# Squared token factors where MLP results are added, and both halves of the tokens in one 512-column matmul

## The chip, the cores and the metric

The kernel runs on one core of one Trainium2 chip. The metric is device time in microseconds (us) of one execution of the whole program; the profile is that of one execution. Engines: TensorE (PE; its weight loads are shown apart as PEld), VectorE (DVE), ScalarE (ACT), GpSimd (POOL), and SyncE (SP), which here only issues DMAs.

## The reference

A decoder trunk of two layers for 256 tokens of width 2048, in float32. Each layer is a mixer (first a gated linear recurrence, then dilated attention) and an MLP; each of the four blocks norms its input and adds its result to the residual `x`:

```python
def _rmsnorm(x, g):
    y = x32 * lax.rsqrt(jnp.mean(x32 * x32, axis=-1, keepdims=True) + EPS)
    return (y * g.astype(jnp.float32)).astype(x.dtype)

def _mlp(h, w1, w2):
    u = jnp.einsum('bsd,df->bsf', h, w1)
    u = jnp.square(jax.nn.relu(u))
    return jnp.einsum('bsf,fd->bsd', u, w2)

x = x + _mlp(_rmsnorm(x, mlp_norm[i]), mlp_w1[i], mlp_w2[i])
```

`w1` is 2048 x 8192, `w2` 8192 x 2048. The norm's factor of a token, call it r, is one number for each token. Since it is positive, relu(r v)^2 = r^2 relu(v)^2, and `w2` acts within a token, so the factor may come in before the relu, as r, or at the end, as r squared.

## The kernel before

**Precision.** A float32 product is made of three products in a faster format: each operand is cut into a high part (`hilo`, `hi_piece`: ACT copies and rounds) and a low part (`lo_piece`: DVE subtracts the high part), and high x high, high x low and low x high are added up in PSUM. The weights come from HBM in units of 1 MB (128 x 2048); `cut_hi` (line 132) and `cut_lo` (line 136) cut each one. There are three buffers for high parts, so the high cut of unit i+3 waits until PE has read the high part of unit i for the last time. The high cut is issued right behind an item (`behind_unit`), the low cut two units ahead (`before_unit`).

**Order.** The program is a list of items, in most cases one weight unit each. For every item the loop at the end issues what must be ready before, then the item's matmuls, then the next high cut, then what was put off to this item: `after(n, fn)` runs `fn` n items later. Each engine works through its instructions in exactly the order in which they were issued; a waiting instruction holds all those behind it on its engine.

**The MLP.** `plan_mlp` goes through 8 parts of 1024 hidden columns. For each part there are eight *first products*, one for each 128 of its hidden columns (`plan_first`, `stand_w`): 16 blocks of 128 inputs, and for each the high weights by the tokens' high part, the high weights by the low part, and the low weights by the high part, three matmuls of 256 columns. The tokens (`xT`) are not normed here, only multiplied by the norm's gains. `u_done` (line 592) takes the sum from PSUM on DVE: relu, times the tokens' factors, which `rstd_rows` has spread over all partitions by two transposes on PE and a copy on ACT. ACT squares it and copies the high part; `u_low` makes the low part one item later.

The *second products* of parts 0 to 6 are made by a scheme with fewer multiplications: a 2 x 2 block product (two token halves, two halves of the part's hidden columns, two chunks of 512 outputs) with seven products instead of eight, on sums of tokens (`sums_of_tokens`, DVE) and sums of weights (line 682 on DVE, and DMAs that add, issued by POOL). Each product is 12 matmuls of 512 columns. Where a product is finished, `take` (line 686) adds it to or takes it from the residual `xc` on DVE. Part 7 goes the plain way (`plan_plain`, `add_x`).

First products of part p+1 are interleaved with second products of part p in an order written out by hand (`ORDER`). Numbered, with W1 to W8 for the first products, it is for each part:

```
W1, b11 0, t1 0, W2, b21 0, b22 0, t2 0, W3, t3 0, W4, t4 0, b11 1, t1 1, W5,
b22 1, t2 1, W6, t3 1, b21 1, W7, W8, t4 1
```

"0" and "1" are the two pairs of output chunks. Seven parts of each of the two MLPs have this form (in part 0, t1 0 and W2 change places), so there are 14 of them, and 12 steps from one to the next. `b22 1` goes on adding in the bank that `t1 1` has written, after its take. A part's token sums are made after `t3 1` of the part before and, for the last pair of hidden columns, after `t4 1`.

**Banks.** A first product writes 256 of the 512 columns of its PSUM bank. For part 0 these are `acc` banks (four, lines with `acc`), later `g` banks (two, used in turn).

`stand_both` is used by the attention for its heads: for each 128 inputs, one matmul of 512 columns has the high weights by both parts of the tokens, and one of 256 the low weights by the high part; `qk_done` copies the half with the low part on ACT and `qk_sum` adds the other.

`add_x`, `close_chunk` and `final_add` add a block's finished result to the residual; `rstd_cols` works out the factors by token (`rs`), one column for each half of the tokens.

Of the kernel before, what the change touches and what calls it, by code (L numbers as in the profile page):

```python
# [9 lines left out]

F32 = mybir.dt.float32
F32R = mybir.dt.float32r
# [10 lines left out]
HD = 128  # L23
DFF = 8192
EPS = 1e-6
KD = D // 128
KR = DR // 128
NCH = D // 512
# [48 lines left out]
def trunk(ctx: ExitStack, tc: tile.TileContext, a: dict, out: bass.AP):  # L77
# [113 lines left out]
    def after(n, fn, *args):  # L191
        later.setdefault(now[0] + n, []).append((fn, args))
# [79 lines left out]
    def new_ssq():  # L272
        state["ssq"] = perm.tile([P, NT, NCH], F32, name="ssq", bufs=2)

    def rstd_cols():
        v = perm.tile([P, 4, NT], F32, name="rs", bufs=2)
        nc.vector.tensor_reduce(v[:, 0, :], state["ssq"], axis=AX.X, op=OP.add)
        nc.vector.tensor_scalar(v[:, 0, :], v[:, 0, :], 1.0 / D, EPS, op0=OP.mult, op1=OP.add)
        nc.scalar.activation(v[:, 1, :], v[:, 0, :], AF.Sqrt)
        nc.vector.reciprocal(v[:, 2, :], v[:, 1, :])  # L280
        nc.vector.tensor_mul(v[:, 3, :], v[:, 2, :], v[:, 2, :])
        nc.vector.tensor_mul(v[:, 3, :], v[:, 3, :], v[:, 0, :])
        nc.vector.tensor_scalar(v[:, 3, :], v[:, 3, :], -0.5, 1.5, op0=OP.mult, op1=OP.add)
        nc.vector.tensor_mul(v[:, 2, :], v[:, 2, :], v[:, 3, :])
        state["rstd"] = v[:, 2, :]

    def rstd_rows():
        state["kick"] = True
# [22 lines left out]
            mm(ps, hi[:, s], xl, False, False)  # L311
            mm(ps, lo[:, s], xh, False, last and j == len(ks) - 1)

    def stand_both(ps, u):

        hi, lo = split[u]
        state["kick"] = False
        for k in range(KD):
            x, s = xT(k), slice(k * 128, (k + 1) * 128)
            mm(ps, hi[:, s], x.rearrange("p (t u q) -> p u q t", t=2, u=2), k == 0, False)  # L320
            mm(ps[:, :S], lo[:, s], moving(x, 0), False, k == KD - 1)

# [42 lines left out]
        for t in range(NT):  # L365
            nc.vector.tensor_add(xc[n][:, t, :], xc[n][:, t, :], acc[t])

    def close_chunk(n, gname, rows):
        def closed(acc):
            if n == 0:  # L370
                new_ssq()
            add_x(n, acc)
            if n < NCH - 1:
                square_sum(n)
            after(1, transpose_chunk, n, gname)
            if n == NCH - 1:
                after(1, square_sum, n)
                after(1, rstd_cols)
                if rows:
                    after(4, rstd_rows)  # L380
        return closed
# [142 lines left out]
    def plan_rec():  # L524
        def proj(h, j, g):
            u = unit(a["w_in"][(KR if g else 0) + 2 * h + j] if len(units) >= FIRST else a["w_first"][len(units)])

            done = gb_done if g else xb_done
            if u < FIRST:
                first[u] = (done, h, j)  # L530
                return

            bank = []

            def begin():
                bank.append(acc_tile() if u > ROWS + 1 else psum.tile([P, 512], F32, name="g" if u <= ROWS else "tr", bufs=2))
                if u == ROWS:
                    stand_w(bank[0][:, :S], u, range(0, HEAD), 0, True, False)
                    state.pop("rows")()

            def run():
                if u != ROWS:
                    begin()
                at = HEAD if u == ROWS else 0
                stand_w(bank[0][:, :S], u, range(at, KD), at, at == 0, True)
                if u == ROWS - 1:
                    first.append((done, h, j, bank[0]))
                else:
                    after(0, done, h, j, bank[0])
            if u == ROWS:  # L550
                item(None, begin)
            item(u, run)

        def gate(h):
            u = unit(a["w_g"][h], 1024)
            item(u, lambda: gate_run(h, u))

        def oproj(n, kq):
            u = unit(a["w_out"][n * 5 + kq])
            out_item(("o", n), u, aT, range(4 * kq, 4 * kq + 4), kq == 0, kq == 4,  # L560
                     close_chunk(n, "mlp0", True))

        for h in range(NB):
            proj(h, 0, 0)
            proj(h, 1, 0)
            proj(h, 0, 1)
            proj(h, 1, 1)
            if h:
                gate(h - 1)
        for kq in (0, 1, 2):  # L570
            oproj(0, kq)
        gate(NB - 1)
        oproj(0, 3)
        for kq in (0, 1, 2, 3):
            oproj(1, kq)
        oproj(0, 4)
        oproj(1, 4)
        for n in (2, 3):
            for kq in range(5):
                oproj(n, kq)  # L580
# [6 lines left out]
    def u_done(p, j, ps):  # L587
        h, k = divmod(j, 4)
        if h == 0:
            squares[p, k] = lru.tile([P, 2, S], F32, name="uu", bufs=4)  # L590
        uu = squares[p, k][:, h, :]
        nc.vector.scalar_tensor_tensor(uu, ps[:, :S], 0.0, state["rstdB"], op0=OP.max, op1=OP.mult)
        nc.scalar.activation(uu, uu, AF.Square)
        t = new_aT(8 * (p % 2) + j)
        nc.scalar.activation(t[:, 0:256], uu, AF.Copy)
        after(1, u_low, t, uu)
        if h == 1 and GROUPS[p]:
            after(1, waiting.append, (p, k))

    def u_low(t, uu):  # L600
        nc.vector.tensor_sub(t[:, 256:512], uu, t[:, 0:256].bitcast(F32))
# [36 lines left out]
    def plan_mlp(w1, w2, done):  # L638
        def plan_first(p, j):
            u = unit(w1[8 * p + j])  # L640

            def run():
                accs["u", p, j] = acc_tile() if p == 0 else psum.tile([P, 512], F32, name="g", bufs=2)
                stand_w(accs["u", p, j][:, :S], u, range(KD), 0, True, True)
                after(0, u_done, p, j, accs.pop(("u", p, j)))
            item(u, run, "w")

        def plan_start():
            us = [unit(w1[j]) for j in (0, 4)]
            for at, ks in enumerate((range(0, 12), range(12, 16))):  # L650
                for u, j in zip(us, (0, 4)):
                    def run(u=u, j=j, ks=ks, at=at):
                        if at == 0:
                            accs["u", 0, j] = acc_tile()
                        stand_w(accs["u", 0, j][:, :S], u, ks, ks[0], at == 0, at == 1)
                        if at == 1:
                            after(1 if j == 0 else 0, u_done, 0, j, accs.pop(("u", 0, j)))
                    item(u, run)

        def plan_plain(p, n, h, last_part):  # L660
            u = unit(w2[((p // 2) * 4 + n) * 4 + (p % 2) * 2 + h])
            out_item(("m", n), u, aT, range(8 * (p % 2) + 4 * h, 8 * (p % 2) + 4 * h + 4), h == 0, h == 1,
                     done(n) if last_part else (lambda acc, n=n: add_x(n, acc)))

        def plan_group(p, n0, last_group):

# [15 lines left out]
                nc.vector.tensor_add(q[to], q[a], q[b])  # L682

            def take(n, t, b, sign):
                x = xc[n0 + n][:, t, :]
                (nc.vector.tensor_add if sign > 0 else nc.vector.tensor_sub)(x, x, bank[b])

            def product(name, loads, source, what, b, first, takes):
                def load_all():
# [197 lines left out]
    def plan_att():  # L887
        def v(g, kq):
            u = unit(a["w_v"][g * 4 + kq])
            out_item(("v", g), u, xT, range(4 * kq, 4 * kq + 4), kq == 0, kq == 3, lambda acc: v_done(g, acc))  # L890

        def head(h):
            for w in range(2):
                def run(u=unit(a["w_qk"][NH * w + h]), w=w):
                    ps = acc_tile()
                    stand_both(ps, u)
                    after(0, qk_done, h, w, ps)
                item(len(units) - 1, run, "w")

        for kq in (0, 1, 2):  # L900
            v(0, kq)
        for kq in (0, 1, 2):
            v(1, kq)
        v(0, 3)
        v(1, 3)
        for h in range(NH):
            if h == NH // 2:
                for g in (2, 3):
                    for kq in range(4):
                        v(g, kq)  # L910
            head(h)

        def oproj(n, kq):
            u = unit(a["w_o"][n * 4 + kq])
            out_item(("a", n), u, aT, range(4 * kq, 4 * kq + 4), kq == 0, kq == 3, close_chunk(n, "mlp1", True))

        for n in (0, 1):
            for kq in (0, 1, 2):
                oproj(n, kq)
        oproj(0, 3)  # L920
        oproj(1, 3)
        for n in (2, 3):
            for kq in range(4):
                oproj(n, kq)


    def final_done(n):
        def done(acc):
            if n == 0:
                new_ssq()  # L930
            add_x(n, acc)
            square_sum(n)
            nc.gpsimd.tensor_mul(xc[n], xc[n], state["gB"][:, None, n * 512:(n + 1) * 512].to_broadcast([P, NT, 512]))
            if n == NCH - 2:
# [11 lines left out]
    def final_add(acc, bank, cols, square, t=0):  # L946

        x = xc[LAST][:, t, cols]
        nc.vector.tensor_add(x, x, acc[bank][:, cols])
        junk = perm.tile([P, 512], mybir.dt.bfloat16, name="junk")  # L950
        nc.scalar.activation(junk[:, cols], x, AF.Square, accum_out=square)

# [88 lines left out]
    plan_rec()  # L1041
    item(None, lru.close)
    item(None, lambda: lru.open("mlp"))
    plan_mlp(a["w1_0"], a["w2_0"], lambda n: close_chunk(n, "mix1", True))
    item(None, lru.close)
    item(None, open_att)
    plan_att()
# [196 lines left out]
```

## Time and profile before

| | us |
|---|---|
| median of 3 runs | 2014.77 (2014.06 to 2015.1) |
| the profiled execution | 2014.87 |
| its span, first to last instruction | 2013.1 |
| granted TensorE clock, mean | 0.998 of full speed |
| weight cuts, high (ACT, 2048 wide) | 1.92 each |
| weight cuts, low (DVE, 2048 wide) | 2.29 each |
| line 592, relu and factor (DVE) | 0.42 each, 128 of them |
| line 686, takes (DVE) | 0.68 each, 150 of them |

The first MLP begins at about 357 us of the span and the second at about 1362; each lasts some 650 us. A row of the timeline gives the start and the length in us, the engine, the line, the operation, the tile written and those read; in square brackets stands how long the engine was idle before, and what ended the wait. A row of the groups ends with the busy time in us, the mean in ns and the idle time before. A row of a source line gives the least, the median and the longest duration in ns and the first and last start. PE's instructions overlap, so the start of one to the start of the next is what one costs; the same goes for DVE and ACT, where it is some 0.08 us less than the duration.

### The profile page before, as it was taken

To read this page: it belongs to the slowest core of one execution; us is meant where nothing else is said; L and a number is where in the kernel's file an instruction comes from. 1 tells how busy PE (TensorE), PEld (TensorE's weight loads), DVE (VectorE), ACT (ScalarE), POOL (GpSimd) and SP (SyncE) were. 2 spreads that over 40 slices of the span, in tenths; PEclk is the share of its full clock that TensorE was granted. 3 is DMA by queue.
4 is the path that set the end of the run, shared out by engine and by line. 5 is a ranking of instruction groups with operands and counts; after the bars stand their busy time and mean duration, and the time that the engine had idled before them with its cause. 6 is when DMAs were issued, how large, how long until landed. Compare 5 with 4: busy or idle time off the path is not lost.

```text
span 2013.1 us, 32932 instructions
## 1 busy us (share of the span) xinstructions
PE 2001.9 (99%) x13761; PEld 1876.5 (93%) x13761; DVE 1721.5 (86%) x1903; ACT 1294.2 (64%) x1420; POOL 87.9 (4%) x83
## 2 busy tenths in 40 slices
PE   9999999999999999999999999999999999999998
PEld 8999988999999999999889999889999999999997
DVE  7999865699999999998658969857999999999985
ACT  7878875566566666665657657656666666666664
POOL 0111110000000000000000000000000000000001
PEclk9999999999999999999999999999999999999999
DMA  8555565688788788787555555456887887887774
GB/s 311 205 195 201 190 225 189 244 258 251 251 287 264 234 288 274 247 250 250 201 210 180 184 194 179 177 194 245 251 251 258 287 269 226 294 276 243 251 242 164
DMA packets 68917, 472.54 MB, mean 235 GB/s; under 512 B 7584, under 2 KB 7712, under 8 KB 13472
## 3 DMA queue, kind: packets, MB, share of 16 engines
q1 hardware_dynamic: 60416, 411.18, 54.3%
q0 software_dynamic: 8064, 58.72, 14.8%
q8 instruction: 108, 1.77, 0.3%
q10 hardware_dynamic: 288, 0.52, 0.1%
q14 instruction: 41, 0.34, 0.0%
HBM read 409.58 MB, written 2.10 MB: 205 GB/s over the span
## 4 chain that ended last, share of the span: by engine, by line
PE 96%; DVE 3%; ACT 0%; issue 0%; DMA 0%; SPq 0%; ACTq 0%
PE acc L201 46%; PE g L201 32%; PE tr L201 18%; DVE wlo L136 1%; PE tr L242 1%; DVE c L437 0%; DMA raw<-in_w_first 0%; ACT whi L132 0%; PE tr L855 0%; DVE c L433 0%; DVE sT L625 0%; DVE qT L682 0%; DVE gw L462 0%; ACT xc L973 0%; DVE i L515 0%
## 5 line engine op out<-in xcount | busy, mean ns | idle before, releaser
L132 ACT ACTIVATE whi<-raw 128x2048 fp32r<-128x2048 f32 (+1 forms) x309 | 568.9, 1844 | 308.8 <-PE acc L201 166.1
L136 DVE TENSOR_TENSOR wlo<-raw,whi 128x2048 fp32r<-128x2048 f32 (+1 forms) x309 | 677.7, 2196 | 94.3 <-ACT whi L132 94.0
L201 PE MATMUL g<-xT,whi 128*128 128x256 f32 x3649 | 617.0, 275 | 0.0
L201 PEld LDWEIGHTS g<-xT,whi 128*128 128x128 f32 x3649 | 554.0, 192 | 0.0
L201 PE MATMUL g<-xT,wlo 128*128 128x256 f32 x1824 | 502.9, 276 | 0.2 <-DVE wlo L136 0.2
L201 PE MATMUL acc<-xT,whi 128*128 128x256 f32 (+1 forms) x2212 | 455.3, 300 | 0.7 <-ACT whi L132 0.7
L201 PE MATMUL acc<-xT,wlo 128*128 128x256 f32 x1360 | 373.3, 274 | 0.7 <-DVE wlo L136 0.6
L201 PEld LDWEIGHTS acc<-xT,whi 128*128 128x128 f32 x2212 | 355.5, 191 | 15.1 <-ACT whi L132 1.8
L201 PEld LDWEIGHTS g<-xT,wlo 128*128 128x128 f32 x1824 | 350.1, 192 | 1.5 <-DVE wlo L136 0.4
L201 PE MATMUL acc<-whi,aT 128*128 128x512 f32 (+1 forms) x1086 | 322.9, 374 | 0.0
L136 DVE TENSOR_TENSOR wlo<-q,whi 128x2048 fp32r<-128x2048 f32 x112 | 255.9, 2285 | 28.0 <-ACT whi L132 27.8
L132 ACT ACTIVATE whi<-q 128x2048 fp32r<-128x2048 f32 x112 | 214.6, 1917 | 79.4 <-PE g L201 52.3
L201 PEld LDWEIGHTS acc<-xT,wlo 128*128 128x128 f32 x1360 | 261.1, 192 | 1.6 <-DVE wlo L136 1.5
L201 PEld LDWEIGHTS acc<-whi,aT 128*128 128x128 f32 x1086 | 204.0, 189 | 27.6
L201 PE MATMUL tr<-whi,sT 128*128 128x512 f32 (+1 forms) x728 | 212.7, 364 | 0.0
L201 PE MATMUL acc<-wlo,aT 128*128 128x512 f32 (+1 forms) x536 | 200.8, 376 | 0.0
L132 ACT ACTIVATE whi<-qT 128x2048 fp32r<-128x2048 f32 x56 | 107.5, 1919 | 127.8 <-PE g L201 93.3
L201 PEld LDWEIGHTS tr<-whi,sT 128*128 128x128 f32 x728 | 137.6, 189 | 20.5
L201 PE MATMUL tr<-whi,aT 128*128 128x512 f32 (+1 forms) x462 | 140.3, 373 | 0.0
L136 DVE TENSOR_TENSOR wlo<-qT,whi 128x2048 fp32r<-128x2048 f32 x56 | 128.0, 2286 | 1.3 <-ACT whi L132 1.3
L201 PE MATMUL tr<-wlo,sT 128*128 128x512 f32 x336 | 127.4, 379 | 0.0
L201 PEld LDWEIGHTS acc<-wlo,aT 128*128 128x128 f32 x536 | 101.1, 189 | 13.2
(170 smaller groups left out, 2144.4 us busy)
## 6 DMA issues: line engine op xcount, KB each, us to landing
raw<-in_w SPq DMA_DIRECT2D x172, 1024.0 KB, 7.0
q<-in_w SPq DMA_DIRECT2D x84, 1024.0 KB, 8.1
raw<-in_w_in SPq DMA_DIRECT2D x35, 1024.0 KB, 4.8
raw<-in_w_qk SPq DMA_DIRECT2D x32, 1024.0 KB, 4.8
q<-q POOLq DMA_DIRECT2D x28, 1024.0 KB, 12.5
q<-qT POOLq DMA_DIRECT2D x28, 1024.0 KB, 7.6
raw<-in_w_out SPq DMA_DIRECT2D x20, 1024.0 KB, 4.8
raw<-in_w_v SPq DMA_DIRECT2D x16, 1024.0 KB, 4.8
```

Source lines behind the costliest of these rows:

```text
L132: nc.scalar.activation(split[i][0][:, s], r, AF.Copy)
L136: nc.vector.tensor_sub(split[i][1][:, s], r, split[i][0][:, s].bitcast(F32))
L201: nc.tensor.matmul(o, l, r, start=start, stop=stop, skip_group_check=True)
L242: nc.tensor.transpose(tr[:, k, t * 128:(t + 1) * 128], xc[n][:, t, c:c + 128], ident)
```

## The change

Two things change in both MLPs.

The first product is made by `stand_both`, 32 matmuls instead of 48, into all 512 columns of its bank. Line 592 becomes three steps in two items: ACT copies the half with the tokens' low part to `uu`, right behind the matmuls; DVE adds the other half and cuts below at zero (TENSOR_ADD_SAT, an operation of DVE's own table: the sum of two tensors, cut above and below at two constants); in the next item ACT squares and makes the high part, and one item after that DVE makes the low part.

The tokens' factors no longer come in there. `rstd_cols` squares them instead (two more small operations, the second for the negative), and every place where an MLP result is added to the residual multiplies by the factor of the token: `take`, the plain adds, the chunk's last add and the final adds. `rstd_rows` is no longer called ahead of the MLPs.

```diff
-    def rstd_cols():
-        v = perm.tile([P, 4, NT], F32, name="rs", bufs=2)
+    def rstd_cols(squared=False):
+        v = perm.tile([P, 6, NT], F32, name="rs", bufs=2)
...
+        if squared:
+            nc.vector.tensor_mul(v[:, 4, :], v[:, 2, :], v[:, 2, :])
+            nc.vector.tensor_scalar(v[:, 5, :], v[:, 4, :], -1.0, None, op0=OP.mult)
+            state["rstd2"] = v[:, 4:6, :]
...
-    def stand_both(ps, u):
+    def stand_both(ps, u, ks=range(KD)):
...
-        for k in range(KD):
+        for k in ks:
...
+    def add_scaled(x, acc, t, sign=1):
+
+        i = 0 if sign > 0 else 1
+        nc.vector.scalar_tensor_tensor(x, acc, state["rstd2"][:, i, t:t + 1], x, op0=OP.mult, op1=OP.add)
+
+    def add_mlp(n, acc):
+        for t in range(NT):
+            add_scaled(xc[n][:, t, :], acc[t], t)
+
-    def close_chunk(n, gname, rows):
+    def close_chunk(n, gname, add):
+        rows = add is add_mlp
+
...
-            add_x(n, acc)
+            add(n, acc)
...
-                after(1, rstd_cols)
+                after(1, rstd_cols, not rows)
                 if rows:
                     after(4, rstd_rows)
...
     def u_done(p, j, ps):
...
-        nc.vector.scalar_tensor_tensor(uu, ps[:, :S], 0.0, state["rstdB"], op0=OP.max, op1=OP.mult)
+        nc.scalar.activation(uu, ps[:, S:], AF.Copy)
+        after(0, u_sum, p, j, ps, uu)
+
+    def u_sum(p, j, ps, uu):
+        nc.vector._custom_dve(TENSOR_ADD_SAT, out=uu, in0=ps[:, :S], in1=uu, s0=LARGEST, s1=0.0)
+        after(1, u_square, p, j, uu)
+
+    def u_square(p, j, uu):
+        h, k = divmod(j, 4)
         nc.scalar.activation(uu, uu, AF.Square)
         t = new_aT(8 * (p % 2) + j)
         nc.scalar.activation(t[:, 0:256], uu, AF.Copy)
         after(1, u_low, t, uu)
         if h == 1 and GROUPS[p]:
-            after(1, waiting.append, (p, k))
+            waiting.append((p, k))
...
-                stand_w(accs["u", p, j][:, :S], u, range(KD), 0, True, True)
-                after(0, u_done, p, j, accs.pop(("u", p, j)))
+                stand_both(accs["u", p, j], u)
+                u_done(p, j, accs.pop(("u", p, j)))
...
             def take(n, t, b, sign):
-                x = xc[n0 + n][:, t, :]
-                (nc.vector.tensor_add if sign > 0 else nc.vector.tensor_sub)(x, x, bank[b])
+                add_scaled(xc[n0 + n][:, t, :], bank[b], t, sign)
...
     def final_add(acc, bank, cols, square, t=0):
...
-        nc.vector.tensor_add(x, x, acc[bank][:, cols])
+        add_scaled(x, acc[bank][:, cols], t)
```

The first two first products of an MLP, each made in two items (`plan_start`), change in the same way.

More of the change, by code (lines that the diff above doesn't have):

```diff
@@ L9 @@
 from concourse._compat import with_exitstack
+from concourse.dve_ops import TENSOR_ADD_SAT
 F32 = mybir.dt.float32
@@ L25 @@
 EPS = 1e-6
+LARGEST = float(np.finfo(np.float32).max)
 KD = D // 128
@@ L560, in oproj @@
             out_item(("o", n), u, aT, range(4 * kq, 4 * kq + 4), kq == 0, kq == 4,
-                     close_chunk(n, "mlp0", True))
+                     close_chunk(n, "mlp0", add_x))
         for h in range(NB):
@@ L654, in run @@
                             accs["u", 0, j] = acc_tile()
-                        stand_w(accs["u", 0, j][:, :S], u, ks, ks[0], at == 0, at == 1)
+                        stand_both(accs["u", 0, j], u, ks)
                         if at == 1:
-                            after(1 if j == 0 else 0, u_done, 0, j, accs.pop(("u", 0, j)))
+                            u_done(0, j, accs.pop(("u", 0, j)))
                     item(u, run)
@@ L662, in plan_plain @@
             out_item(("m", n), u, aT, range(8 * (p % 2) + 4 * h, 8 * (p % 2) + 4 * h + 4), h == 0, h == 1,
-                     done(n) if last_part else (lambda acc, n=n: add_x(n, acc)))
+                     done(n) if last_part else (lambda acc, n=n: add_mlp(n, acc)))
         def plan_group(p, n0, last_group):
@@ L914, in oproj @@
             u = unit(a["w_o"][n * 4 + kq])
-            out_item(("a", n), u, aT, range(4 * kq, 4 * kq + 4), kq == 0, kq == 3, close_chunk(n, "mlp1", True))
+            out_item(("a", n), u, aT, range(4 * kq, 4 * kq + 4), kq == 0, kq == 3, close_chunk(n, "mlp1", add_x))
         for n in (0, 1):
@@ L930, in done @@
                 new_ssq()
-            add_x(n, acc)
+            add_mlp(n, acc)
             square_sum(n)
@@ L1043, in trunk @@
     item(None, lambda: lru.open("mlp"))
-    plan_mlp(a["w1_0"], a["w2_0"], lambda n: close_chunk(n, "mix1", True))
+    plan_mlp(a["w1_0"], a["w2_0"], lambda n: close_chunk(n, "mix1", add_mlp))
     item(None, lru.close)
```

## The prediction

> **What bounds the kernel now.** I read the page first, then the waits, then one period of the MLP on the timeline of each engine.
>
> ```profile
> PE 2001.9 (99%) x13761; PEld 1876.5 (93%) x13761; DVE 1721.5 (86%) x1903; ACT 1294.2 (64%) x1420; POOL 87.9 (4%) x83
> PE 96%; DVE 3%; ACT 0%; issue 0%; DMA 0%; SPq 0%; ACTq 0%
> ```
>
> TensorE (PE) is busy 99% of the span and carries 96% of the chain that ended last, so over the whole span a shorter matmul stream is worth its full length. The table by stretches shows how near a second engine is in the stage that changes:
>
> ```profile
> 500.00:600.00 100.00, 100.00 (x704) 94.29 (x703) 93.33 (x82) 63.33 (x53) 4.28 (x5) 1.00 0.81 268
> ```
>
> The columns are PE, PEld, DVE, ACT, POOL. VectorE (DVE) works 93.33 of 100 us there, ScalarE (ACT) 63.33. The idle 7% is not spread evenly: it lies behind two of the eight first products of a part, W3 and W6. From each, DVE runs without a pause until PE itself waits for it. I call these **stretch A** (end of W3 to product b22 1) and **stretch C** (end of W6 to W2 of the next part). Stretch A on the timelines of PE, ACT and DVE:
>
> ```profile
> 509.78 0.38 PE L201 MATMUL tr<-whi,sT 128*128 128x512 f32 x1
> 509.87 1.91 ACT L132 ACTIVATE whi<-q 128x2048 fp32r<-128x2048 f32 x1 [3.32 <-PE g L201]
> 509.98 0.42 DVE L592 SCALAR_TENSOR_TENSOR uu<-g,rstdB 128x256 f32<-128x256 f32 x1 [0.71 <-PE g L201]
> 511.81 2.29 DVE L136 TENSOR_TENSOR wlo<-q,whi 128x2048 fp32r<-128x2048 f32 x1 [1.41 <-ACT whi L132]
> 530.12 0.68 DVE L686 TENSOR_TENSOR xc<-xc,tr 128x512 f32<-128x512 f32 x1
> 530.76 0.28 PE L201 MATMUL g<-xT,wlo 128*128 128x256 f32 x1
> 530.95 0.45 PE L201 MATMUL tr<-whi,sT 128*128 128x512 f32 x1
> ```
>
> W3 ends at 509.78. The high cut that needs its weight buffer starts then on ACT; DVE takes the low cut at its end (511.81), runs on to a take that ends at 530.80, and PE, which would have begun b22 1 0.11 us after 530.76, begins at 530.95: it waited 0.08 us for that take, whose bank b22 1 adds to. Stretch C:
>
> ```profile
> 541.57 0.38 PE L201 MATMUL tr<-whi,sT 128*128 128x512 f32 x1
> 541.66 1.92 ACT L132 ACTIVATE whi<-raw 128x2048 fp32r<-128x2048 f32 x1 [3.32 <-PE g L201]
> 543.61 2.29 DVE L136 TENSOR_TENSOR wlo<-raw,whi 128x2048 fp32r<-128x2048 f32 x1 [1.41 <-ACT whi L132]
> 568.59 2.28 DVE L136 TENSOR_TENSOR wlo<-raw,whi 128x2048 fp32r<-128x2048 f32 x1
> 570.92 0.38 PE L201 MATMUL g<-xT,wlo 128*128 128x256 f32 x1
> ```
>
> W6 ends at 541.57; DVE's run ends with the low cut of W2 at 570.87, and PE uses it at 570.92, its first use, a wait of about 0.08 us like that in A. Both come back in every part; first and last of 14 for A and of 12 for C:
>
> ```profile
> 451.43 0.45 PE L201 MATMUL tr<-whi,sT 128*128 128x512 f32 x1
> 1933.85 0.45 PE L201 MATMUL tr<-whi,sT 128*128 128x512 f32 x1
> 491.40 0.38 PE L201 MATMUL g<-xT,wlo 128*128 128x256 f32 x1
> 1894.31 0.38 PE L201 MATMUL g<-xT,wlo 128*128 128x256 f32 x1
> ```
>
> So PE and DVE are level to a tenth of a microsecond at 26 places. PE time saved inside A or C is a wait there, and time added to these two runs is paid in full. That decides the change.
>
> **What PE saves.** One pair of first products back to back (96 matmuls of 256 columns), and one pair of attention heads, which use stand_both already:
>
> ```profile
> 546.75 0.39 PE L201 MATMUL g<-xT,whi 128*128 128x256 f32 x2
> 557.48 0.38 PE L201 MATMUL tr<-whi,aT 128*128 128x512 f32 x1
> 1094.62 0.38 PE L201 MATMUL acc<-xT,whi 128*128 128x512 f32 x1
> 1105.10 0.38 PE L855 MATMUL tr<-con,s 128*128 128x128 f32 x2
> ```
>
> 10.73 us against 10.48: 0.125 us for each of 128 first products, 16.0 us in all. The columns streamed are the same; what goes is one of three matmul starts in a row of 128 inputs, 0.125/16 = 7.8 ns each.
>
> The Trainium skill ("TensorE: Matmul & The Clock Gate", section "Wait — 56ns, not 53.3ns?") gives a fixed cost of about 2.5 ns per warm matmul over its columns. By that rule the saving would be 16 × 2.5 = 40 ns a product, 5.1 us in all, and the change dearer than I forecast; the trace's 7.8 ns disagrees, and I use it.
>
> **What is put into the two runs.**
>
> (1) *The copy of the low half.* It is issued inside the item, so ahead of the next high cut on ACT, and reads the whole bank. The rows 509.87 and 509.98 show that the weight buffer is free 0.11 us before the bank is complete. How soon a high cut follows such a copy:
>
> ```profile
> 1082.06 0.39 ACT L781 ACTIVATE y<-acc 128x256 f32<-128x256 f32 x1
> 1082.34 1.91 ACT L132 ACTIVATE whi<-raw 128x2048 fp32r<-128x2048 f32 x1
> ```
>
> 0.28 us. The cut behind W3 and W6, and DVE's run with it, starts 0.11 + 0.28 = 0.39 us later. DVE has only the sum to do meanwhile, and it idles 1.41 us there already. The other copies cost nothing: ACT has 37% to spare and the cuts behind them are ahead of DVE. Queued behind each copy are high cuts and the squares; behind the sum, which now waits for PE and then for ACT, the low cuts. Within the runs DVE is late by more than the copy, so those sums wait for nothing.
>
> (2) *The takes*, an add that becomes a multiply-add with a factor per token. That form stands in the trace, from PSUM, at line 777; two of them, then the next instruction, and one take with its next:
>
> ```profile
> 1163.29 1.40 DVE L777 SCALAR_TENSOR_TENSOR av<-acc,rs,av 128x512 fp32r<-128x512 f32 x2
> 1164.61 4.48 DVE L136 TENSOR_TENSOR wlo<-raw,whi 128x2048 fp32r<-128x2048 f32 x2
> 484.01 0.68 DVE L686 TENSOR_TENSOR xc<-xc,tr 128x512 f32<-128x512 f32 x1
> 484.61 0.42 DVE L601 TENSOR_TENSOR aT<-uu,aT 128x256 fp32r<-128x256 f32 x1
> ```
>
> 0.66 against 0.60 us: 0.06 each. Grouped by line, the takes of A (511.5 to 530.5) and of C (543.3 to 568.5) are
>
> ```profile
> L686 DVE TENSOR_TENSOR xc<-xc,tr 128x512 f32<-128x512 f32 x4 | 2.7, 679 | 0.0
> L686 DVE TENSOR_TENSOR xc<-xc,tr 128x512 f32<-128x512 f32 x2 | 1.4, 680 | 0.0
> ```
>
> so A grows by 0.24 and C by 0.12 us. The takes outside, and the adds in the last part, lie beside PE.
>
> (3) *The sum of both halves* (TENSOR_ADD_SAT) replaces line 592, once in A and three times in C. No row has this operation. Nearest are the two-operand add from PSUM, and at the far end the scan, which takes two steps for an element:
>
> ```profile
> L785 DVE TENSOR_TENSOR y<-y,acc x32: 403/405/414, 1054.0 to 1282.0; 128x256 f32<-128x256 f32 x32
> L592 DVE SCALAR_TENSOR_TENSOR uu<-g,rstdB x112: 411/417/426, 406.8 to 1961.1; 128x256 f32<-128x256 f32 x112
> L515 DVE TENSOR_TENSOR_SCAN i<-a,c 128x256 f32<-128x256 f32 x20 | 12.7, 679 | 0.3
> ```
>
> Between −0.01 and +0.26 us each; I take 0, since it too is one pass with two operands.
>
> (4) *Square and low part one item later.* The number of low parts inside A and C stays two and three. The square of W8 moves behind a high cut, but the token sums that read it stand on DVE, which is behind PE by more than that there: 0.
>
> (5) *One wait goes.* In A the low cut after W4's line 592 starts 0.41 us behind it, where the instruction after one without a wait follows at 0.34:
>
> ```profile
> 519.36 0.42 DVE L592 SCALAR_TENSOR_TENSOR uu<-g,rstdB 128x256 f32<-128x256 f32 x1
> 519.77 2.29 DVE L136 TENSOR_TENSOR wlo<-qT,whi 128x2048 fp32r<-128x2048 f32 x1
> 567.65 0.42 DVE L592 SCALAR_TENSOR_TENSOR uu<-g,rstdB 128x256 f32<-128x256 f32 x1
> 567.99 0.68 DVE L625 TENSOR_TENSOR sT<-sw,sT 128x512 fp32r<-128x512 f32 x1
> ```
>
> It waited 0.07 us for its high cut, and a later run finds that done. A: 0.39 + 0.24 − 0.07 = 0.56 us. C: 0.39 + 0.12 = 0.51.
>
> (6) *Start and end.* Per MLP the transposes of rstd_rows go from PE,
>
> ```profile
> 368.73 0.38 PE L291 MATMUL tr<-con,rs 128*128 128x128 f32 x2
> 368.86 0.58 PE L201 MATMUL acc<-xT,whi 128*128 128x128 f32 x3
> ```
>
> 0.13 us each, 0.26. The two small DVE operations for the squared factors and the dropped row copy lie beside PE. The last token half's final add is on the path to the output: +0.06. DMA issues, their order and POOL's and SP's queues stay.
>
> **The sum.** Inside A lie W4 and W5, so PE arrives 2 × 0.125 = 0.25 us earlier and waits 0.56 + 0.25 = 0.81 us longer; 14 times, 11.3 us. Inside C lie W7, W8 and W1: 0.51 + 0.375 = 0.885; 12 times, 10.6 us. Together 21.9 of new waiting against 16.0 of saved matmuls and 0.26 − 0.06 = 0.2: **+5.7 us**. The profiled execution took 2014.87 us (span 2013.1), 0.10 above the median 2014.77 of the three runs; 2014.87 + 5.7 = 2020.6, by the median 2020.5. I forecast **2020.5 us**.
>
> **The rivals.**
> - *PE's gain arrives whole*: the late starts at 530.95 and 570.92 are PE's own turn from one shape to the other, and DVE's runs could end later unnoticed. For it, PE's 96% of the chain; against it, that the take ends at 530.80 and the cut at 570.87, just ahead of both starts. With a slack of s at each place the time is 2020.5 − 26 s; from s = 0.22 us nothing is lost, and from 0.885 all is gained: 2014.8 − 16.2 = 1998.6 us.
> - *The copy is hidden*, because the high cut behind W3 and W6 keeps its start: 26 × 0.39 = 10.1 us less than my sum, 2010.4 us. Against it, the order of issue on ACT.
> - *The sum is a slow instruction*, like the scan: 0.26 us once in A and three times in C, 14 × 0.26 + 36 × 0.26 = 13.0 us more, 2033.5 us. It decides from 0.05 us a sum (2.5 us more). Nothing speaks for it but that the operation is unknown.
> - *The 512-column form saves only 2.5 ns a matmul start* here, where other traffic shares SBUF: 0.04 us a product. A then waits 0.56 + 0.08, C 0.51 + 0.12: 9.0 + 7.6 = 16.6, less 5.1 and 0.2: +11.3, 2026.1 us. This is the rule named above; the heads' rows speak against it.
>
> **How the numbers follow.** Forecast 0.67, gain whole 0.10, copy hidden 0.08, slow sum 0.10, small saving 0.05. About 0.2% (4 us) is what a measurement of this kernel can tell from no change. The forecast's own bounds: the delay from 0.28 (the copy starts with the cut's old release) to 0.5 us is −2.9 to +2.9; a sum from −0.01 to +0.06 us is −0.5 to +3.0; so 2017 to 2026.5, and I put 0.15 of its 0.67 within 4 us. The hidden copy lies at the edge, half same, half faster. Faster 0.10 + 0.04 = 0.14; same 0.15 + 0.04 = 0.19; slower 0.52 + 0.10 + 0.05 = 0.67. The range leaves out the whole gain and the slow sum, 0.20: 2010 to 2027 us.
>
> **What would show it.** First products' pairs at 10.48 us; the high cut behind W3 about 0.5 us after its end instead of 0.09; takes at 740 ns; PE standing some 0.8 us at b22 1 and at W2's second matmul, so a part takes 79.5 − 3 × 0.125 + 0.56 + 0.51 = 80.2 us where it took 79.5 (451.43 to 530.95). PE without waits at both places would prove me wrong, and so would a period below 79 us.

## The result and the profile after

The changed kernel takes 2024.24 us (median of 4 runs, 2023.52 to 2025.45) beside 2014.74 (median of 4, 2014.06 to 2015.1) for the one before: ratio 1.0048, 95% interval 1.0036 to 1.006. It is 9.5 us slower; 5.7 were forecast (2020.5 us). The profiled execution took 2023.52 us, its span is 2021.7, and the clock was 0.999, so all the time below is at the same clock as before.

From the page after, engine totals and the chain that ended last; then the table by stretches for the same 100 us as before (PE, PEld, DVE, ACT, POOL):

```profile
PE 1993.7 (99%) x11705; PEld 1802.4 (89%) x11705; DVE 1729.0 (86%) x1907; ACT 1319.0 (65%) x1546; POOL 87.6 (4%) x83
PE 61%; DVE 28%; issue 6%; ACT 4%; DMA 1%; SPq 0%; ACTq 0%; DVEq 0%
```

```profile
500.00:600.00 100.00, 98.95 (x542) 88.20 (x541) 92.95 (x81) 64.26 (x63) 4.29 (x5) 1.00 0.81 264
```

The totals hardly move (DVE 86% in both), and by them nothing has happened. The chain tells it: PE carried 96% before and carries 61% now, DVE 28%. In the 100 us PE is no longer busy throughout: 1.05 us are missing.

PE's timeline shows the saving that was expected, and where it goes. A pair of first products, W7 and W8, first row to second; then b22 1 in three parts, one period apart:

```profile
548.39 0.38 PE L203 MATMUL g<-xT,whi 128*128 128x512 f32 x1
558.87 0.38 PE L203 MATMUL tr<-whi,aT 128*128 128x512 f32 x1
...
452.49 0.45 PE L203 MATMUL tr<-whi,sT 128*128 128x512 f32 x1 [0.18 <-DVE xc L377]
532.70 0.46 PE L203 MATMUL tr<-whi,sT 128*128 128x512 f32 x1 [0.18 <-DVE xc L377]
612.91 0.45 PE L203 MATMUL tr<-whi,sT 128*128 128x512 f32 x1 [0.18 <-DVE xc L377]
```

The pair takes 10.48 us, as forecast (10.73 before), and the part 80.21 us (79.52 before). Over 32 blocks of 128 inputs that is 0.335 us a block before, for three matmuls of 256 columns, and 0.3275 after, for one of 512 and one of 256. An estimate from the Trainium skill ("TensorE: Matmul & The Clock Gate", section "Wait — 56ns, not 53.3ns?") would have been a saving of 0.04 us a product, from 2.5 ns for each matmul start. The pair gives 0.125, or 7.8 ns for each start that goes. The 7.8 ns are those of this exchange of shapes; no run shows that each matmul start costs as much.

What PE waits for now. In stretch A, at t1 1 and b22 1; in stretch C, at W2's second matmul:

```profile
523.80 0.38 PE L203 MATMUL tr<-whi,aT 128*128 128x512 f32 x1
524.44 0.45 PE L203 MATMUL tr<-whi,sT 128*128 128x512 f32 x1 [0.26 <-DVE xc L377]
524.74 0.38 PE L203 MATMUL tr<-wlo,sT 128*128 128x512 f32 x1
...
532.25 0.27 PE L203 MATMUL g<-xT,wlo 128*128 128x256 f32 x1
...
572.08 0.38 PE L203 MATMUL g<-xT,whi 128*128 128x512 f32 x1
573.06 0.38 PE L203 MATMUL g<-xT,wlo 128*128 128x256 f32 x1 [0.60 <-DVE wlo L138]
```

Matmuls of 512 columns follow each other here at 0.215 us. 523.80 to 524.44 is 0.64, so PE stood 0.43, and the next start comes 0.08 late as well (0.30). At b22 1 it is 0.345 and 0.075. Together 0.925 where the kernel before stood 0.155: A costs 0.77 more. In C the second matmul is 0.77 late; with 0.18 of short stands at t1 0 that is 0.95 against 0.08: 0.87 more (the 0.10 behind W2's late start is the same in both kernels). 14 × 0.77 + 12 × 0.87 = 21.2 us.

What stands in front of DVE at W3: the end of W3 on PE (the next product's first row), then ACT, then DVE:

```profile
511.00 0.38 PE L203 MATMUL tr<-whi,sT 128*128 128x512 f32 x1
```

```profile
511.20 0.38 ACT L609 ACTIVATE uu<-g 128x256 f32<-128x256 f32 x1 [3.31 <-PE g L203]
511.48 1.91 ACT L134 ACTIVATE whi<-q 128x2048 fp32r<-128x2048 f32 x1
```

```profile
511.61 0.42 DVE L613 CUSTOM_DVE_ANT_0 uu<-g,uu 128x256 f32<-128x256 f32 x1 [1.08 <-ACT uu L609]
513.41 2.29 DVE L138 TENSOR_TENSOR wlo<-q,whi 128x2048 fp32r<-128x2048 f32 x1 [1.38 <-ACT whi L134]
523.55 0.74 DVE L377 SCALAR_TENSOR_TENSOR xc<-tr,rs,xc 128x512 f32<-128x512 f32 x1
531.81 0.74 DVE L377 SCALAR_TENSOR_TENSOR xc<-tr,rs,xc 128x512 f32<-128x512 f32 x1
```

The copy goes first, and the high cut (L134) follows 0.28 us behind it, 0.48 behind W3's end where it was 0.09. DVE's run starts at its end, 513.41, and has no gap up to the take that ends at 532.55. PE follows 0.15 later, and 0.15 after the take at 523.55 too: both ends of waits are takes. Grouped, the takes; and one source line's answer for the sum:

```profile
L377 DVE SCALAR_TENSOR_TENSOR xc<-tr,rs,xc 128x512 f32<-128x512 f32 x140 | 104.3, 745 | 0.0
```

```profile
L613 DVE CUSTOM_DVE_ANT_0 uu<-g,uu x112: 411/418/426, 408.0 to 1970.3; 128x256 f32<-128x256 f32 x112
```

A take went from 679 to 745 ns; the new sum takes what line 592 took, 418 against 417.

**Part 0.** Here PE waited for nothing before, and now stands in two places of the first MLP (and at the second of them in the other MLP, 1.49 us). PE's rows, then DVE's. q12 is one of the weight units of the second products; `sw` are token sums:

```profile
406.88 0.38 PE L203 MATMUL tr<-wlo,aT 128*128 128x512 f32 x1
408.09 0.38 PE L203 MATMUL tr<-whi,aT 128*128 128x256 f32 x1 [0.83 <-DVE aT L626]
...
418.83 0.38 PE L203 MATMUL acc<-whi,sT 128*128 128x512 f32 x1
420.48 0.48 PE L203 MATMUL acc<-wlo,sT 128*128 128x512 f32 x1 [1.26 <-DVE wlo L138]
```

```profile
386.48 0.43 DVE L637 TENSOR_TENSOR sw<-uu 128x256 f32<-128x256 f32 x1 [1.68 <-ACT uu L618]
398.08 2.29 DVE L707 TENSOR_TENSOR qT<-raw,q 128x2048 f32<-128x2048 f32 x1 [4.35 <-DMA q<-in_w]
...
418.14 2.28 DVE L138 TENSOR_TENSOR wlo<-q,whi 128x2048 fp32r<-128x2048 f32 x1
```

PE is 0.99 late at the first and 1.42 at the second, with 0.1 more just behind each. Ahead of this DVE is not full: it stands for ACT's square and for the load of q12, which lands at 398.0, where in the kernel before it landed at 396.7. From 398.08 on DVE has no gap up to the end of the low cut at 420.42, and PE takes that cut at 420.48. The same load, the same low cut and PE's first use of it in the kernel before:

```profile
396.79 2.29 DVE L682 TENSOR_TENSOR qT<-raw,q 128x2048 f32<-128x2048 f32 x1 [1.97 <-DMA q<-in_w]
417.09 2.28 DVE L136 TENSOR_TENSOR wlo<-q,whi 128x2048 fp32r<-128x2048 f32 x1
419.93 0.38 PE L201 MATMUL acc<-wlo,sT 128*128 128x512 f32 x1
```

There the low cut ended at 419.37, 0.56 us before PE used it: DVE was nearly level with PE here too.

Adding, over both MLPs, all by which a matmul starts later than its kind does without a wait: 4.7 us before, 29.5 after. 24.8 new less 16.2 saved is 8.6, the difference of the two spans (2021.7 and 2013.1). So the trace leaves nothing over; the experiments ask why each wait is as long as it is.

### The profile page after: what moved, and what is told of

Read it like the earlier page. It is cut to its first block, busy times and chain, and to the rows that moved or that the text cites. A ratio compares the mean times of both kernels' runs of the same rounds, so it can differ in the third digit from the quotient of the medians.

```text
span 2021.7 us, 28903 instructions
## 1 busy us (share of the span) xinstructions
PE 1993.7 (99%) x11705; PEld 1802.4 (89%) x11705; DVE 1729.0 (86%) x1907; ACT 1319.0 (65%) x1546; POOL 87.6 (4%) x83
## 4 chain that ended last, share of the span: by engine, by line
PE 61%; DVE 28%; issue 6%; ACT 4%; DMA 1%; SPq 0%; ACTq 0%; DVEq 0%
PE acc L203 40%; DVE wlo L138 14%; PE g L203 14%; PE tr L203 6%; DVE qT L707 5%; ACT whi L134 3%; DVE xc L377 2%; DVE sT L650 1%; DVE aT L626 1%; DVE uu L613 1%; DVE sw L637 1%; DMA q<-in_w 1%; DVE sw L638 1%; DVE sw L640 1%; PE tr L244 1%
## 5 line engine op out<-in xcount | busy, mean ns | idle before, releaser
L134 ACT ACTIVATE whi<-raw 128x2048 fp32r<-128x2048 f32 (+1 forms) x309 | 568.9, 1843 | 224.8 <-PE acc L203 146.9
L203 PE MATMUL g<-xT,whi 128*128 128x512 f32 (+2 forms) x1857 | 603.9, 378 | 0.0
L203 PEld LDWEIGHTS g<-xT,whi 128*128 128x128 f32 x1857 | 348.8, 189 | 44.3
L203 PEld LDWEIGHTS g<-xT,wlo 128*128 128x128 f32 x1824 | 350.1, 192 | 10.8 <-DVE wlo L138 10.8
L203 PEld LDWEIGHTS acc<-xT,whi 128*128 128x128 f32 x1952 | 325.2, 191 | 21.4 <-ACT whi L134 1.5
L134 ACT ACTIVATE whi<-q 128x2048 fp32r<-128x2048 f32 x112 | 214.2, 1913 | 22.2 <-PE tr L203 11.6
L609 ACT ACTIVATE uu<-g 128x256 f32<-128x256 f32 x112 | 42.5, 380 | 220.9 <-PE g L203 220.9
L134 ACT ACTIVATE whi<-qT 128x2048 fp32r<-128x2048 f32 x56 | 107.4, 1917 | 51.5 <-DVE qT L707 49.6
```

What stands on the lines that cost most here:

```text
L134: nc.scalar.activation(split[i][0][:, s], r, AF.Copy)
L203: nc.tensor.matmul(o, l, r, start=start, stop=stop, skip_group_check=True)
L609: nc.scalar.activation(uu, ps[:, S:], AF.Copy)
```

## The experiments

Times are medians, with the ratio to the kernel before, measured again beside each group of versions (2014.95 to 2015.54). "Theory" is that PE's saving is real, that only DVE's time inside A and C is paid, and that PE waits for the end of these runs.

**Takes as plain adds** (the factor of the MLP norms is left out):

```diff
-        nc.vector.scalar_tensor_tensor(x, acc, state["rstd2"][:, i, t:t + 1], x, op0=OP.mult, op1=OP.add)
+        (nc.vector.tensor_add if sign > 0 else nc.vector.tensor_sub)(x, x, acc)
```

> The changed kernel (2024.2 us) with the takes and MLP adds as plain adds again; the factor of the MLP norms is left out of the computation altogether. Two-run theory (only DVE time between the end of W3 and b22 1, and between the end of W6 and W2, is paid): the takes in A fall by 4 x 0.06 and in C by 2 x 0.06 us, 14 x 0.24 + 12 x 0.12 = 4.8 us less, 2019.4 us; PE's waits at t1 1 and b22 1 shrink by 0.24 together, that in W2 by 0.12. Rival, all DVE time is paid (DVE is the bound everywhere in the MLP): 165 adds x 0.06 = 9.9 us less, 2014.3 us. Rival, the longer takes lie beside PE: no difference, 2024.2 us.

2018.79 us, ratio 1.0018 (1.0009 to 1.0027), period 79.83. The takes are worth 5.4 us of the 9.5, as the theory had it.

**The factors alone**: the first product and its sum as before (48 matmuls, one pass for the relu), only the takes changed.

```diff
-        nc.scalar.activation(uu, ps[:, S:], AF.Copy)
-        after(0, u_sum, p, j, ps, uu)
...
+        nc.vector.tensor_scalar(uu, ps[:, :S], 0.0, None, op0=OP.max)
```

> The kernel before with the second part of the change alone: stand_w as before, relu without the factor, the squared factors in the takes and adds, no rstd_rows ahead of the MLPs. Two-run theory: PE saves nothing, ACT copies nothing, and the takes lengthen the runs by what the plain takes gave back (0.25 in A, 0.18 in C): 14 x 0.25 + 12 x 0.18 - 0.3 = 5.4 us over before (2014.9), 2020.3 us. Rival, all DVE time is paid: 165 x 0.06 = 9.9 us, 2024.8 us. Rival, the factors cost nothing where DVE is not late: 2014.9 us.

2018.34 us, 1.0017 (1.0008 to 1.0026). This half of the change makes the kernel slower by itself, 3 us where 5 were expected, and PE waits for nothing in part 0. The waits there belong to the other half.

**Copy of the low half on DVE behind W3 and W6**, so that the high cut starts at once; DVE idles there. In the code W1 to W8 have `j` = 0, 4, 1, 5, 2, 6, 3, 7, so W3 and W6 are 1 and 6:

```diff
-        nc.scalar.activation(uu, ps[:, S:], AF.Copy)
+        if p and j in (1, 6):
+            nc.vector.tensor_copy(uu, ps[:, S:])
+        else:
+            nc.scalar.activation(uu, ps[:, S:], AF.Copy)
```

> The changed kernel with the copy of the low half made by DVE instead of ACT, for W3 and W6 alone, so that the high cut behind them starts when the weight buffer is free. Two-run theory: both runs start 0.39 us earlier, the copy (0.34 us more work for DVE) fits into the 1.4 us in which DVE idles there: 26 x 0.39 = 10.1 us less, 2014.1 us; the high cut behind W3 starts 0.1 us after its end. Rival, DVE is the bound everywhere: 28 x 0.34 = 9.5 us more, 2033.7 us. Rival, the copy is not what delays: 2024.2 us.

2017.6 us, 1.0014 (1.0005 to 1.0024), period 79.73: 6.6 us gained of 10.1. C gained its 0.39; A gained 0.1. DVE's timeline in A:

```profile
520.01 0.42 DVE L616 CUSTOM_DVE_ANT_0 uu<-g,uu 128x256 f32<-128x256 f32 x1
520.62 2.29 DVE L138 TENSOR_TENSOR wlo<-qT,whi 128x2048 fp32r<-128x2048 f32 x1 [0.19 <-ACT whi L134]
```

The run starts earlier and then stands for the high cut behind W4, which W4's own copy still holds back on ACT. In the changed kernel DVE comes too late there to notice.

**A second pass over the result of the sum**, which changes no value, first behind W3 and W6, where DVE idles next, then (`j` 3 and 7) behind W7 and W8, inside C:

```diff
+        if p and j in (1, 6):
+            nc.vector.tensor_tensor(uu, uu, uu, op=OP.max)
```

> The changed kernel with one more DVE operation of 0.34 us (the maximum of uu and uu, which changes nothing) behind the sums of W3 and W6. Two-run theory: these two stand in front of the runs, in DVE's idle 1.4 us: 0 +- 0.5 us, 2024.2 us. Rival, DVE is the bound everywhere: 28 x 0.34 = 9.5 us more, 2033.7 us.

> The same operation behind the sums of W7 and W8 instead, the same number of them. Two-run theory: both stand inside C, of which there are 12: 12 x 2 x 0.34 = 8.2 us more, 2032.4 us, all of it in PE's wait in W2. Rival, DVE is the bound everywhere: 9.5 us more, 2033.7 us, and no difference to the run with W3 and W6. Rival, nothing of it is paid: 2024.2 us.

Behind W3 and W6: 2023.54 us, 1.0041 (1.0026 to 1.0056), the changed kernel's time. Behind W7 and W8: 2034.26 us, 1.0094 (1.0077 to 1.0111), 10 us more. Twice the same 28 instructions: outside the stretches they cost nothing, inside C (24 of them) 10 us. DVE's timeline of the second:

```profile
558.63 0.42 DVE L613 CUSTOM_DVE_ANT_0 uu<-g,uu 128x256 f32<-128x256 f32 x1
559.08 0.42 DVE L615 TENSOR_TENSOR uu<-uu 128x256 f32<-128x256 f32 x1
559.42 0.69 DVE L652 TENSOR_TENSOR sT<-sw,sT 128x512 fp32r<-128x512 f32 x1
```

The pass that reads the sum starts 0.45 behind it, and the next, independent one 0.34 behind the pass. So a pass adds 0.45 us and not the 0.34 of the expectation: 24 × 0.45 = 10.8, where 8.2 were expected and 10 measured.

**Low parts later.** If DVE's work in the stretches is what costs, moving some out should gain. Four of the eight low parts of a part (`u_low`) are put off until the stretch is over, in the changed kernel (below) and in the kernel before, where each number is one higher:

```diff
-        after(1, u_low, t, uu)
+        put_off = {1: 4, 5: 2, 6: 6, 7: 2} if 0 < p < 7 else {1: 4, 5: 2} if p else {}
+        after(put_off.get(j, 1), u_low, t, uu)
```

> The changed kernel (2024.2 us) with four low parts (u_low, 0.34 us each on DVE) issued later: those of W3 and W4 behind the take of t1 1, so out of A, those of W6 and W8 behind the low cut of W2, so out of C. DVE's work is the same. Two-run theory: A and C shorten by 0.68 us each, 26 x 0.68 = 17.7 us less, 2006.5 us, a little more if the moved work makes PE wait elsewhere. Rival, DVE is the bound everywhere and moved work is paid where it lands: 2024.2 us.

> The kernel before with the same four low parts issued at the same later places. Two-run theory: its runs are late by only 0.16 us in A and 0.08 us in C, so no more than that can be gained: 14 x 0.16 + 12 x 0.08 = 3.2 us less, 2011.7 us. Rival, the order of the low parts is worth its full 0.68 us by itself: 17.7 us less, 1997 us. Rival, those waits are PE's own: 2014.9 us.

Changed kernel: 2015.34 us, 1.0001 (0.9992 to 1.0011). Kernel before: 2011.7 us, 0.9981 (0.9972 to 0.9991), and no wait of PE is left in its parts. So the kernel before could be made faster by ending its two short waits. The changed kernel gained 8.9 us of the 17.7 expected: the wait at b22 1 is gone, but 0.34 at t1 1, 0.28 at W2 and 0.34 at b22 0, whose low cut now has the moved parts ahead of it, stay.

**Both remedies, and token sums later in part 0**:

> The changed kernel with the later low parts, the copy behind W3 and W6 on DVE, and, in the part before the interleaved ones, token sums one item later. Two-run theory: A and C are about 1.0 us shorter than in the changed kernel, which waits 0.93 and 0.95 us there, so PE waits at neither place any more and its 16 us arrive: 2014.9 - 16.2 = 1998.7 us, and up to 4 us more if the waits in part 0 remain. Rival, DVE is the bound everywhere: 2024 us or more. Rival, moved work makes PE wait in b21 0 or b22 0: 2003 to 2010 us.

2014.79 us, 0.9996 (0.9986 to 1.0005): the wait at b22 0 that the rival named came, and t1 1's stayed, but the time is outside the rival's 2003 to 2010 us as well. The period is 79.18, the first of a changed kernel below 79.52, yet the time is not better: part 0 got worse. The later sums came too late for the product that reads them, and PE stood 2.85 and 2.2 us for them. They are no remedy. The first wait of part 0, though, fell from 0.99 to 0.28 us in the first MLP, and from 0.09 to nothing in the second.

**The load of q12 early in part 0** (asked for in the item of `j` 5, W4 of part 0):

```diff
+                if p == 0 and j == 5:
+                    early.pop()()
...
+            if p == 0 and n0 == 0:
+                early.append(lambda: fetch("q12", 0, 1, "q12"))
```

> The changed kernel, but in part 0 of each MLP the 1 MB of q12 is asked for in the item of W's j = 5, some three items earlier than it was, so SP's queue has it ahead of two of the other loads. Theory: the waits ahead of product t1 0 and in part 0 (1.0 and 1.5 us in the first MLP, 0.1 and 1.6 in the second) come from DVE, which stands 4.35 us for the landing of q12 at 398.0 and is late from there on. With q12 there by 393 the sum starts about 2.5 us earlier, these waits go, and the time is 2024.2 - 4.2 = 2020.0 us. Rival: the stretch from 390 to 410 us is bound by its loads as a whole (DMA share 0.93 and 0.85, the last q lands at 403), so another load or cut takes the place of this one and PE waits as long: 2024.2 us. Second rival: DVE's order is the limit (token sums behind ACT's squares), with q12 early DVE's next wait is there: half of it, about 2022.

2023.46 us, 1.0039 (1.0025 to 1.0053). DVE, then PE:

```profile
394.61 2.28 DVE L716 TENSOR_TENSOR qT<-raw,q 128x2048 f32<-128x2048 f32 x1
408.40 0.42 DVE L637 TENSOR_TENSOR sw<-uu 128x256 f32<-128x256 f32 x1 [1.68 <-ACT uu L618]
```

```profile
407.41 0.59 PE L203 MATMUL tr<-whi,aT 128*128 128x512 f32 x2
420.60 0.48 PE L203 MATMUL acc<-wlo,sT 128*128 128x512 f32 x1 [1.52 <-DVE wlo L138]
```

The sum of weights starts at 394.61 instead of 398.08, without a wait, and PE's first wait is gone. The second is 0.26 us longer, so 0.8 of the 4.2 us came: nearest to the first rival, that something else takes the load's place. DVE has time in hand now, and loses it where the token sums of the last pair stand 1.68 us for ACT's square, issued an item later than it was and behind a high cut. So part 0 has two causes in a row. In the changed kernel DVE runs from q12's landing to both waits; with q12 early, by these rows, the square's place holds DVE nearly as long (408.40 for 408.29 in the changed kernel), and the second wait stays.

**Copies behind the high cuts** of W3, W4 and W6, with sum, square and low part an item later:

```diff
+        if p and j in (1, 5, 6):
+            after(0, u_copy, ps, uu)
+            after(1, u_sum, p, j, ps, uu)
+            return
```

> The changed kernel, but for W3, W4 and W6 of a part the copy of the low half is issued behind the high cut instead of ahead of it, and sum, square and low part come one item later than they did. Nothing is added to DVE's work. Theory: the copy ahead of the high cut costs 0.39 us in each of A and C, and what kept A from gaining when DVE made the copies of W3 and W6 was W4's own copy. So both stretches get 0.39 back: 2024.2 - 26 x 0.39 = 2014.1 us, and the period falls from 80.2 to 79.4. Rival: in A another wait stays (as with the copies on DVE, where A gained 0.1): 2024.2 - 12 x 0.39 - 14 x 0.1 = 2018.1 us, period 79.7.

2024.49 us, 1.0045 (1.003 to 1.006): no gain, against theory and rival. ACT and DVE in A:

```profile
511.42 1.91 ACT L134 ACTIVATE whi<-q 128x2048 fp32r<-128x2048 f32 x1 [3.20 <-PE g L203]
513.24 0.37 ACT L617 ACTIVATE uu<-g 128x256 f32<-128x256 f32 x1
```

```profile
513.37 2.29 DVE L138 TENSOR_TENSOR wlo<-q,whi 128x2048 fp32r<-128x2048 f32 x1 [2.50 <-ACT whi L134]
518.44 0.41 DVE L620 CUSTOM_DVE_ANT_0 uu<-g,uu 128x256 f32<-128x256 f32 x1
521.26 2.29 DVE L138 TENSOR_TENSOR wlo<-qT,whi 128x2048 fp32r<-128x2048 f32 x1 [0.21 <-ACT whi L134]
```

The expectation said that nothing is added to DVE's work. That holds for the kernel and not for the stretch: W3's sum, which in the changed kernel lay at 511.61 in DVE's idle time, stands at 518.44 inside the run, 0.33 us. Another low part fell out at the end, and 0.21 of waiting for W4's high cut came in. Where an instruction lies decides, once more, not how many there are.

**These copies, q12 early and two low parts later**:

> Copies behind the high cuts for W3, W4 and W6, q12 early in part 0, and two of the low parts moved out of the stretches: W3's from A (three items behind its square) and W8's from C (two items behind its square); one low part more than that was moved out of C in the earlier version. Theory: A has 0.42 us of new waiting left after the copies and loses 0.34 of DVE work, C has 0.5 left and loses 0.34, so some 0.1 to 0.2 us a stretch are left, 4 us in all, and PE's 16.2 us come through but for these: 2014.9 - 16.2 + 4 = 2002.7 us. Rival: the waits found behind them stay (t1 1 for the take of t4 0, b22 0 for its low cut, 0.3 to 0.4 us each): 14 x 0.85 = 11.9 us, 2010.6 us, no better than the kernel before with four low parts later (2011.7).

2021.87 us, 1.0032 (1.002 to 1.0043). It missed in part for the same reason: the sums of W3 and W6 are inside the stretches. In C, DVE also stands 0.45 us for a high cut (at 553.06), which it did not in the changed kernel.

**A last version** puts together what had gained and what the rows pointed to: copies of W3 and W6 on DVE in its idle time, W4's behind its high cut, W3's and W8's low parts later, q12 early, and in part 0 the last pair's square right behind its sum.

```diff
+        if p and j in (1, 6):
+            nc.vector.tensor_copy(uu, ps[:, S:])
+        elif p and j == 5:
+            after(0, u_copy, ps, uu)
+            after(1, u_sum, p, j, ps, uu)
+            return
...
+        if p == 0 and j == 7:
+            u_square(p, j, uu)
...
+        put_off = {1: 4, 7: 2} if 0 < p < 7 else {1: 4} if p else {}
```

> The version with the copies of W3 and W6 on DVE and low parts later (2014.8 us), with three changes aimed at the waits it had left. (a) W4's copy goes behind its high cut and its sum, square and low part come one item later: the low cut that waited 0.53 us for that high cut no longer does, and with it goes the wait of 0.41 us at t1 1: 14 x 0.41 = 5.8 us. (b) only W8's low part is moved out of C, not W6's too: of the 0.44 us at b22 0 some 0.1 stays, with as much again in C: 12 x 0.25 = 3 us. (c) in part 0 q12 comes early, the token sums come as in the changed kernel, and the last pair's square is made right behind its sum, so that DVE no longer stands 1.68 us for it: of some 5 us of waits in the two part 0's 2 to 3 are left. Theory, that DVE's run in each stretch is all that counts: 2014.8 - 5.8 - 3 - 2.5 = 2003.5 us, faster than the kernel before with four low parts later (2011.7). Rival: with a wait gone the next one behind it is as long (as every step so far has found one): 2011 to 2015 us.

2008.57 us, 0.9964 (0.995 to 0.9978): faster than both kernels, between the theory and its rival. The kernel before with low parts later (2011.7 us, 0.9981) is slower by the medians, but the two were not measured side by side and their intervals touch. PE:

```profile
419.49 0.48 PE L203 MATMUL acc<-wlo,sT 128*128 128x512 f32 x1
...
530.16 0.45 PE L203 MATMUL tr<-whi,sT 128*128 128x512 f32 x1 [0.18 <-DVE xc L377]
...
609.30 0.45 PE L203 MATMUL tr<-whi,sT 128*128 128x512 f32 x1 [0.18 <-DVE xc L377]
```

The period is 79.14 us; part 0's second wait is 0.21 us for 1.53, and the first 0.53 for 0.99. Waits at b22 1 (0.42) and at W2 (0.24) remain: over both MLPs starts are 13.4 us late against 4.7 in the kernel before, and 2015.5 + 8.7 − 16.2 = 2008.0. Early q12 and the earlier square were not run apart here.

## Why the prediction was right, and where it fell short

- **What bounds the kernel**: right for the periodic parts. PE and DVE were level at 26 places. DVE time added inside C is paid and the same in front of A and C is not (the second pass: 10 and 0 us); time taken out of A came back only in part, by the next wait.
- **What PE saves**: right, 10.48 us a pair.
- **(1) The copy**: the size is right, the cut comes 0.48 us behind W3's end for 0.09, 0.39 more. Taken away on DVE, it returned in full in C; in A the next wait took most of it, so there its price is what lies behind it.
- **(2) The takes**: 66 ns each for 0.06; with plain adds 5.4 us came back, where 14 × 0.24 + 12 × 0.12 = 4.8 was the estimate.
- **(3) The sum**: right at 0; the rival of a slow instruction is out by the row of 418 ns.
- **(5) A wait that goes** and the **sum per stretch**: the wait went (the low cut behind W4's sum starts at 521.36, 0.34 behind it). 0.81 and 0.885 forecast, 0.77 and 0.87 measured. It lies in another place than foretold: half of A's is at t1 1, and b22 1, where all of it was expected, has 0.42. PE is held by a chain of takes, and the earlier take in it stops PE first.
- **(4) Square and low part an item later: 0.** This step failed. It looked at the periodic parts, where DVE is behind PE and waits for no square. Ahead of part 0 DVE is not behind, and there it stands for the square at the token sums, 1.41 and then 1.68 us (the row at 386.48). Some 6 us later DVE idles 4.35 us for q12, so these stands cost nothing as DVE time. They act through the load: the low cut behind the sums ends later, it frees the buffer of a load, and q12 is asked for right behind that load (389.82 and 390.25). Counted from the MLP's first matmul, q12 is asked for at 32.9 us in the kernel before, at 33.6 in the changed kernel, and at 32.2 in the version with later token sums ("both remedies"), where DVE stands for no square there. How much of PE's standing comes this way was not run apart.
- **What was counted whole.** With (4) fell a tacit step: that the first ten products of each MLP (eight of part 0, then W1 and W2) keep their saving, 1.25 us. In the first MLP PE would use the low cut 1.6 us sooner than before and DVE ends it 1.4 us later, both counted from the MLP's first matmul, and only 0.56 us were to spare. PE stands 2.6 us there and 1.8 in the second MLP, 4.4 together; the rest of the miss is small and of both signs. No bound of the forecast stood for a wait in part 0, so that its range held this one too is luck.
- **(6) Start and end**: 0.2 us, not run apart.

Of the rivals, the gain whole, the hidden copy, the slow sum and the small saving are each refuted by the rows above. That q12 lands 1.3 us later although it was asked for only 0.3 later (390.25 for 389.91) is left open. In the second MLP it takes 6.9 us from request to landing in both kernels, in the first 6.8 before and 7.7 after. The DMA share from 390 to 400 us is 0.94 before and 0.93 after, but what shares out the bandwidth was not tried.

## What to carry to other kernels

Where two engines are level, cutting the work of one is worth only what the other can follow: find its unbroken runs, count each instruction that moves into or out of one of them; the ones put outside cost nothing here. A saving in one wait shows the next, here 0.3 us behind, so look for all the waits of a period together before trusting a sum. Places outside the period, such as the first part, need their own reading: slack and order differ there, and an instruction that waits can cost time through the load whose buffer is freed behind it.

## What the runs showed of the hardware

- A multiply-add with a factor for each partition, from PSUM, costs 745 ns for 512 columns where the two-operand add costs 679.
- On DVE, 256 columns: an instruction that reads the one just before starts 0.45 us behind it, an independent one 0.34.
- In the version with both remedies PE stood 2.2 us at about 1420.7 us, and then the clock fell. The table by stretches (its last three columns are the granted clock, the DMA share and GB/s):

```profile
1424.00:1427.40 3.40, 3.40 (x10) 2.66 (x10) 3.08 (x2) 2.02 (x3) 0.00 (x0) 0.52 1.09 222
```

For 3.4 us the granted clock was 0.52, and matmuls of 512 columns came at 0.427 instead of 0.215 us. The Trainium skill ("TensorE: Matmul & The Clock Gate", section "What's actually happening") has such a gate, with a window of about 3.4 us. The length agrees, but here the pause before it was shorter than a window. In the first MLP of the same run a pause of 2.85 us had no such effect (granted clock 1.00 from 419.0 to 426.0 us).
